# A two-layer hybrid encoder on one core: where the residual gate is applied, a branch projection by column halves, and the router's constant row

## The chip, the core and the metric

The kernel runs on one core of one Trainium2 chip. The metric is the device time of one execution, in microseconds. The core's engines work side by side, each through its own queue in order: TensorE (PE) multiplies matrices and transposes into PSUM banks, VectorE (DVE) and ScalarE (ACT) do elementwise work and move results out of PSUM, GpSimd (POOL) does elementwise work on SBUF, and SyncE (SP) issues the loads. An engine that waits holds up everything behind it in its own queue.

## The reference

Two layers, 256 tokens of 1024 channels. Each layer has a mixer and a mixture of experts; this is the part that the change touches (gt1, sc2 and sh2 come from the conditioning vector):

```python
    y_mla = mla_mixer(...) @ w_br_mla
    y_dil = dilated_mixer(dil_qkv, pos, g_q_dil, g_k_dil) @ w_br_dil
    y_win = window_mixer(win_qkv, pos, g_q_win, g_k_win, sink_win) @ w_br_win
    return (g_mla * y_mla + g_dil * y_dil + g_win * y_win) @ w_out
...
        h = rms_norm(x, g_norm1[l]) * (1 + sc1) + sh1
        x = x + gt1 * hybrid_mixer(h, pos, ...)
        h = rms_norm(x, g_norm2[l]) * (1 + sc2) + sh2
        x = x + gt2 * hier_moe(h, ...)
```

The gate gt1 is one row of 1024 values, so it may scale the columns of w_out or the product. The router takes h, and its logits h @ [w_gr, w_er] are computed as the normalised x times weights scaled by g_norm2 * (1 + sc2), plus a constant row that holds sh2 times the unscaled weights and the router's biases.

## The kernel before

Tokens lie in two tiles of 128 (t = 0, 1), channels in eight tiles of 128 (kt). A mixer is a list of jobs, each with a split and an mm part. A split takes a piece of a weight apart for three-pass multiplication: ScalarE rounds it (kh), VectorE subtracts (kl, L124 in the helper split). The mm part runs, for each token tile and column half, three matmuls: high x high, high x low, low x high. The loop at the end of mixer (L1327 to L1350) sets the order by hand: at job i it first runs the hooks registered for i, then splits some jobs ahead, then the mm part, whose last job of a product also runs its post function. An engine gets its instructions in exactly this order.

The last 18 jobs of a mixer are four for the first branch product (br0), two for the second (br1), four for the third (br2), and eight for the output projection (out); 1024 columns each, in two halves of 512 (j = 0, 1). k_jobs makes them. With halves=True the last two k-steps are run for one column half and then for the other, so that the post of half 0 runs before the matmuls of half 1 end.

- merge(br), L1139 to L1162: multiplies a branch's product by its sigmoid gate (L1156, from PSUM) and adds it into m (L1160, both inputs in SBUF). For br2 all adds are on VectorE; for br1 those of t = 0 are on GpSimd.
- start_out, L1179, a hook before the first out job: transposes all of m (L515; copies L525 on ScalarE, residual parts L526 on VectorE give mH and mL) and between the halves runs router_row (L547): eight matmuls for the constant row on all 128 partitions, an addition, and the scaling of the router weights in place (L556).
- out_gate, L1209, eight hooks from two jobs before the end of br1 on: the first makes the gate rows by gate_rows (L461: two matmuls that spread a row over the partitions, and copies, tile gtb), and each multiplies one 1024-column piece of w_out by the gate, in two GpSimd instructions (L1215).
- post_out, L1195: adds the product to x (L1205) and squares it for the norm.
- moe, L1353: transposes x (tile x2T), normalises, runs the router's logits (tile lg, 2 x 8 matmuls), and a chain of small VectorE instructions picks experts (it starts at L1375). The expert products follow.

Loads are issued by pump whenever a buffer of the ring comes free: branch weights in six units of three pieces (key bo), then the expert weights (key e).

Of the kernel before, what the change touches and what calls it, by code (L numbers as in the profile page):

```python
# [37 lines left out]
class Kern:  # L38
# [62 lines left out]
    def mm(self, out, lhsT, rhs, start, stop):  # L101
        self.nc.tensor.matmul(out, lhsT, rhs, start=start, stop=stop)  # L102
# [49 lines left out]
    def schedule(self, l):  # L152

        keys = []
        for c in range(10):
            keys += [('in', l, c)] * 4
            if c == 4:
                keys += [('uq', l)] * 4
            if c == 5:
                keys += [('ukv', l)] * 2  # L160
        first = len(keys)
        for c in range(10, 18):
            keys += [('in', l, c)] * 4
        last = len(keys)
        keys += [('bo', l, r // 3) for r in range(18)]
        if l == 0:
            keys[:12] = [keys[i] for i in self.FIRST]
        ada = [('ada', l, 1, u) for u in range(6)] + [('ada', l, 2, u) for u in range(6)]
        if l + 1 < self.layers:
            ada += [('ada', l + 1, 0, u) for u in range(6)]  # L170
        at = {}
        steps = []
        for k in ada:
            steps.append(k)
            if k[3] == 5:
                steps += [None, None]
        steps = steps[self.early(l):]
        lo, hi = 14 if l == 0 else 8, last - 5
        for n, k in enumerate(steps):
            at.setdefault(lo + n * (hi - lo) // len(steps), []).append(k)  # L180
        return keys, at
# [55 lines left out]
    def setup(self):  # L237

        nc, a, C = self.nc, self.a, self.const
        nc.scalar.preload_act_table_set(EXP_LN)  # L240
        pk = C('pk', [128, N_PK])
        nc.sync.dma_start(pk, a['pk'])
        self.ccol, self.sel4, self.cols = pk[:, 0:8], pk[:, 8:12], pk[:, 12:68].rearrange("p (l n) -> p l n", l=DEPTH)
        self.ident = pk[:, 68:196]
        self.identb = C('identb', [128, 128], BF)
        self.x = [self.alloc('w', [128, D], F32, 'x') for _ in range(2)]
        self.rows = C('rows', [128, N_ROW + DEPTH * 108])
        nc.sync.dma_start(self.rows, bass.AP(tensor=a['rows'].tensor, offset=a['rows'].offset,
                                             ap=[[0, 128], [1, N_ROW + DEPTH * 108]]))
        self.lrow = self.rows[:, N_ROW:].rearrange("p (l n) -> p l n", l=DEPTH)  # L250
        self.ipos = self.alloc('s', [128, 2 + T], I32, 'ipos')
        nc.sync.dma_start(self.ipos, a['pos'])
        for t in range(2):
            nc.sync.dma_start(self.x[t], a['x'][t])
        self.pump(2)
        self.bz0 = [self.alloc('s', [128, 512], F32, 'bz') for _ in range(2)]
        for h in range(2):
            nc.vector.memset(self.bz0[h], 0.0)
            nc.sync.dma_start(self.bz0[h][0:64:32], a['b_ada'][0, 0][h::2])
        self.sel2 = C('sel2', [128, 2])  # L260
        nc.vector.tensor_add(self.sel2, self.sel4[:, 0:2], self.sel4[:, 2:4])
        self.pump(4)
        self.load_kr(0)
        self.pump()
        nc.vector.tensor_copy(self.identb, self.ident)
        self.eps = C('eps', [128, 1])
        nc.vector.memset(self.eps, EPS)
        self.zero = C('zero', [128, 1])
        nc.vector.memset(self.zero, 0.0)

        t1 = self.small(8)
        nc.scalar.activation(t1, self.ccol, AF.Exp, scale=-1.0)
        nc.vector.tensor_scalar(t1, t1, 1.0, None, op0=ALU.add)
        nc.vector.reciprocal(t1, t1)
        self.cond = C('cond', [128, 8])
        nc.vector.tensor_mul(self.cond, t1, self.ccol)
        self.mod = {}
# [266 lines left out]
            self.free(tmp)  # L544


    def router_row(self, l):  # L547

        nc = self.nc
        ab = self.mod[l, 1]  # L550
        p = self.bank('rr')
        for kt in range(8):
            self.mm(p[:, :36], ab[:, 8 + kt:9 + kt].to_broadcast([128, 128]), self.wr[:, kt], kt == 0, kt == 7)
        self.rrow = self.cp.tile([128, 36], F32, name=f"rrow_{l}", tag='rrow')
        nc.vector.tensor_add(self.rrow, p[:, :36], self.lrow[:, l, 72:108])
        nc.vector.tensor_mul(self.wr, self.wr, ab[:, 0:8, None].to_broadcast([128, 8, 36]))  # L556
        self.free(p)

    def drain(self, g):
# [3 lines left out]
    def mixer(self, l):  # L563
# [48 lines left out]
        def k_jobs(key_of, cols, kts, lhs, post, banks, halves=False):  # L612
# [41 lines left out]
                return split, mm  # L654
            for i in range(kts):
                jobs.append(mk(i))

        self.at = 0
        att = deque()
# [412 lines left out]
        def hook(f):  # L1072
            hooks.setdefault(len(jobs), []).append(f)
# [90 lines left out]
        def bo_key(k0):  # L1164
            def f(i):
                r = k0 + i
                return ('bo', l, r // 3), (r % 3) * 1024, r % 3 == 2
            return f
# [5 lines left out]
            return f  # L1174
        k_jobs(bo_key(0), 1024, 4, lhs_o('oA', 0), merge(0), 'br0')
        k_jobs(bo_key(4), 1024, 2, lhs_o('oA', 4), merge(1), 'br1')
        k_jobs(bo_key(6), 1024, 4, lhs_o('oB', 0), merge(2), 'br2', True)

        def start_out():  # L1179
            self.free(M['oA'], M['oB'], M['G', 0], M['G', 1])  # L1180
            M['mH'] = self.alloc('u', [128, 12, 256], F32R, 'mH')
            M['mL'] = self.alloc('u', [128, 12, 256], F32R, 'mL')
            m = M['m']
            for k0 in (0, 4):
                self.transposed(lambda t, k: m[:, t, (k0 + k) * 128:(k0 + k) * 128 + 128], 4, M['mH'], M['mL'], kt0=k0)
                if k0 == 0:
                    self.router_row(l)
            self.ring = 8
            self.free(M['mg'])
        hook(start_out)  # L1190

        def lhs_m(kt, t):
            return M['mH'][:, kt, t * 128:t * 128 + 128], M['mL'][:, kt, t * 128:t * 128 + 128]

        def post_out(b, js):  # L1195
            if js == (0,):
                self.ss = self.small(4)
                self.free(*M['gt'])
            else:
                self.ring = 10  # L1200
                self.free(M['mH'], M['mL'])
            for j in js:
                for t in range(2):
                    xs = self.x[t][:, j * 512:j * 512 + 512]
                    nc.vector.tensor_add(xs, xs, b[t][j])  # L1205
                    self.squares(self.ss, t, j)
                    self.free(b[t][j])

        def out_gate(i):  # L1209
            if i == 0:  # L1210
                M['gt'] = self.gate_rows(l, 0)
            key, off, _ = bo_key(10)(i)
            u = self.take(key)[:, off:off + 1024]
            for h in range(2):
                nc.gpsimd.tensor_mul(u[:, 512 * h:512 * h + 512], u[:, 512 * h:512 * h + 512], M['gt'][h])  # L1215
        for i in range(8):
            hooks.setdefault(len(jobs) + i - 6, []).append(lambda i=i: out_gate(i))
        k_jobs(bo_key(10), 1024, 8, lhs_m, post_out, 'out', True)

        if l == 0:  # L1220
# [100 lines left out]
        for i in range(nj):  # L1321
            self.at = i
            for f in hooks.pop(i, []):
                f()
            if l == 0 and i == 5:
                next(g2)
                jobs[6][0]()  # L1327
                next(g2)
                late()
                second_half()  # L1330
                split = 9
                self.ring = 3
            while split < min(nj if i >= 5 else nfirst, i + 1 + (DEEP if i < nj - 13 else 2 if i == nj - 9 else 3)):
                jobs[split][0]()
                split += 1
            jobs[i][1]()
            if l == 0 and i in (3, 4):
                next(g2)
            if i in (nj - 11, nj - 4):
                self.load_pieces(l, 2)  # L1340
            credit += RATE
            while att and credit >= 1:
                att.popleft()()
                credit -= 1
            if not att:
                credit = 0.0
            for _ in at.get(i, []):
                next(bg)
# [4 lines left out]
    def moe(self, l):  # L1353
# [1 line left out]
        ab = self.mod[l, 1]  # L1355
        V = nc.vector
        xT = [self.alloc('w', [128, 4, 256], F32, 'x2T') for _ in range(2)]
        self.transposed(lambda t, k: self.x[t][:, k * 128:k * 128 + 128], 8, None, None, full=xT)
        xn, rs = self.norm_x('xn2', self.ss)

        pt = self.bank('lg')
        for t in range(2):
            for kt in range(8):
                self.mm(pt[:, t * 64:t * 64 + 36], xT[kt // 4][:, kt % 4, t * 128:t * 128 + 128], self.wr[:, kt], kt == 0, kt == 7)
        self.free(*xT)
        y = [[self.bank('y') for _ in range(2)] for _ in range(2)]
        for j in range(2):
# [546 lines left out]
```

## Time and profile before

| | us |
|---|---|
| median of 3 runs | 1406.43 |
| lowest and highest | 1405.89, 1408.21 |
| the profiled execution | 1407.64 |
| its span, first to last instruction | 1405.5 |
| TensorE busy in the span | 1336.0 |
| VectorE busy | 683.4 |
| ScalarE busy | 537.3 |
| GpSimd busy | 187.7 |

The profile is of one execution. The span leaves out 2.1 us of that execution's time. A matmul on fp32 data stands in the trace as more than one instruction, and consecutive matmuls overlap: an instruction that lasts 0.39 us may start 0.23 us after the one before. The layers' mixers end at 356 and 1035 us, each followed by 32 experts.

### The profile page before, as it was taken

To read this page: it belongs to the slowest core of one execution; us is meant where nothing else is said; L and a number is where in the kernel's file an instruction comes from. 1 tells how busy PE (TensorE), PEld (TensorE's weight loads), DVE (VectorE), ACT (ScalarE), POOL (GpSimd) and SP (SyncE) were. 2 spreads that over 40 slices of the span, in tenths; PEclk is the share of its full clock that TensorE was granted. 3 is DMA by queue.
4 is the path that set the end of the run, shared out by engine and by line. 5 is a ranking of instruction groups with operands and counts; after the bars stand their busy time and mean duration, and the time that the engine had idled before them with its cause. 6 is when DMAs were issued, how large, how long until landed. Compare 5 with 4: busy or idle time off the path is not lost. (4 is left out here: it accounts for less than half of the span.)

```text
span 1405.5 us, 19475 instructions
## 1 busy us (share of the span) xinstructions
PE 1336.0 (95%) x7662; PEld 877.6 (62%) x7662; DVE 683.4 (49%) x1404; ACT 537.3 (38%) x1134; POOL 187.7 (13%) x170
## 2 busy tenths in 40 slices
PE   5999999998899999999899999999889999999997
PEld 3778787887544444444368988888764444444443
DVE  5587564767623323332256775566863233233222
ACT  4555553563422222221155555456433222222211
POOL 0002064325100000000000203540810000000000
PEclk9999999999999999999999999999899999999999
DMA  9865557267689999999994526516767999999993
GB/s 375 365 248 212 196 211 291 99 270 280 232 348 427 425 425 425 425 425 425 420 414 160 203 90 259 176 76 254 270 239 289 405 425 426 425 425 426 424 424 129
DMA packets 45215, 437.95 MB, mean 312 GB/s; under 512 B 5080, under 2 KB 5608, under 8 KB 11328
## 3 DMA queue, kind: packets, MB, share of 16 engines
q1 hardware_dynamic: 44832, 435.78, 76.5%
q8 instruction: 62, 1.02, 0.3%
q0 software_dynamic: 288, 0.89, 0.2%
q14 instruction: 33, 0.27, 0.1%
HBM read 435.59 MB, written 1.05 MB: 311 GB/s over the span
## 5 line engine op out<-in xcount | busy, mean ns | idle before, releaser
L102 PE MATMUL in<-h,hH 128*128 128x384 f32 (+1 forms) x576 | 206.1, 358 | 3.7 <-ACT hH L1286 2.5
L1631 DVE TENSOR_TENSOR O<-O,gth 64x512 f32<-64x512 f32 (+1 forms) x132 | 88.8, 673 | 241.0 <-PE O L102 240.0
L102 PE MATMUL in<-h,hL 128*128 128x384 f32 (+1 forms) x576 | 195.3, 339 | 0.1
L102 PE MATMUL in<-l,hH 128*128 128x384 f32 (+1 forms) x576 | 194.6, 338 | 0.0
L1570 ACT ACTIVATE u<-A 64x384 f32<-64x384 f32 x64 | 31.1, 486 | 301.2 <-PE A L102 301.2
L102 PEld LDWEIGHTS in<-h,hH 128*128 128x128 f32 x576 | 109.1, 189 | 29.3 <-issue 18.0
L102 PEld LDWEIGHTS in<-h,hL 128*128 128x128 f32 x576 | 108.9, 189 | 1.4 <-DVE hL L1287 1.3
L102 PEld LDWEIGHTS in<-l,hH 128*128 128x128 f32 x576 | 109.3, 190 | 0.5
L1520 ACT ACTIVATE xT<-ga,modab 128x128 f32<-128x128 f32 x256 | 92.8, 467 | 21.0 <-PE ga L102 20.9
L1637 ACT ACTIVATE Op<-O 128x1024 fp32r<-128x1024 f32 x30 | 31.7, 1057 | 138.7 <-DVE O L1631 138.7
L1571 DVE SCALAR_TENSOR_TENSOR u<-A,m,u 64x384 f32<-64x384 f32 x64 | 39.4, 616 | 89.9 <-ACT u L1570 86.2
L743 POOL TENSOR_TENSOR rot<-TB,rope 128x256 f32<-128x256 f32 x8 | 11.7, 1483 | 488.4 <-ACT UC L813 429.0
L102 PE MATMUL ga<-Poh,xp 128*128 128x256 f32 x512 | 71.7, 295 | 0.0
L1540 DVE CAST PTp<-PTe 128x256 fp32r<-128x256 bf16 x32 | 13.6, 425 | 117.4 <-PE PTe L102 117.4
L102 PE MATMUL y<-Op,PTp 128*128 128x512 f32 x240 | 70.2, 415 | 0.0
L102 PEld LDWEIGHTS ga<-Poh,xp 128*128 128x128 f32 x512 | 66.0, 198 | 5.8 <-issue 4.4
L887 ACT ACTIVATE P<-P,m 128x256 f32<-128x256 f32 (+1 forms) x48 | 27.6, 576 | 79.2 <-DVE m L945 37.1
L102 PEld LDWEIGHTS y<-Op,PTp 128*128 128x128 f32 x240 | 40.6, 188 | 21.1 <-issue 15.5
L1638 DVE TENSOR_TENSOR Op<-O,Op 128x1024 fp32r<-128x1024 f32 x30 | 36.8, 1225 | 33.8 <-ACT Op L1637 29.2
L970 POOL TENSOR_SCALAR qz<-UC,gq 128x384 f32<-128x384 f32 x16 | 22.7, 1417 | 142.7 <-PE oT L102 72.6
L973 POOL TENSOR_SCALAR bias<-dist 128x128 f32<-128x128 f32 (+1 forms) x48 | 36.1, 752 | 5.2 <-PE oT L102 1.3
L102 PE MATMUL br<-kh,oA 128*128 128x512 f32 x96 | 31.3, 401 | 0.0
(845 smaller groups left out, 2532.3 us busy)
## 6 DMA issues: line engine op xcount, KB each, us to landing
piece<-in_w_e SPq DMA_DIRECT2D x12, 512.0 KB, 4.1
w('ada', 0, 0, 0)_4_90<-in_w_ada SPq DMA_DIRECT2D x1, 1536.0 KB, 9.5
w('ada', 0, 0, 1)_5_92<-in_w_ada SPq DMA_DIRECT2D x1, 1536.0 KB
w('in', 0, 0)_9_104<-in_w_in SPq DMA_DIRECT2D x2, 768.0 KB, 16.4
w('in', 0, 1)_10_108<-in_w_in SPq DMA_DIRECT2D x2, 768.0 KB, 16.3
w('in', 0, 2)_11_110<-in_w_in SPq DMA_DIRECT2D x2, 768.0 KB, 12.2
w('ada', 0, 0, 3)_18_194<-in_w_ada SPq DMA_DIRECT2D x1, 1536.0 KB
w('ada', 0, 0, 4)_35_250<-in_w_ada SPq DMA_DIRECT2D x1, 1536.0 KB
```

The lines of the kernel that those rows point to most:

```text
L102: self.nc.tensor.matmul(out, lhsT, rhs, start=start, stop=stop)
L743: g.tensor_mul(t[i], x, tab[:, i, :, None, :].to_broadcast([128, 2, nh, 16]))
L887: nc.scalar.activation(dst, src, AF.Exp, bias=mx_neg[:, i:i + 1], scale=1.0, accum_out=sm[:, i:i + 1])
L970: nc.gpsimd.tensor_scalar(qz, M['qd'][:, pr::2, t * 128:t * 128 + 128], self.gq[:, l, 1 + hh:2 + hh], None, op0=ALU.mult)
L973: nc.gpsimd.tensor_scalar(bias[:, lo:hi], self.dist[:, t, 256 + lo:256 + hi], -DIL_SLOPE[g][h], None, op0=ALU.mult)
L1520: nc.scalar.activation(dst, src, AF.Identity, scale=a2[:, kt:kt + 1], bias=s2[:, kt:kt + 1])
L1540: V.tensor_copy(PT[p], pv)
L1570: nc.scalar.activation(u[b:b + 64], A[c:c + 64, :384], AF.Silu)
L1571: V.scalar_tensor_tensor(u[b:b + 64], A[b:b + 64, :384], GC[e // 2][b:b + 64, e % 2:e % 2 + 1], u[b:b + 64], op0=ALU.mult, op1=ALU.mult)
L1631: V.tensor_mul(O[e // 2][b:b + 64, 512 * h + c:512 * h + c + n], o[c][p, :n], gt[p, c:c + n])
L1637: nc.scalar.activation(hi, whole, AF.Copy)
L1638: V.tensor_sub(lo, whole, hi)
```

## The change

Three edits. First, the gate gt1 no longer scales w_out: out_gate and its GpSimd instructions go, and post_out multiplies the product by the gate row on VectorE, from PSUM into an SBUF tile, and adds that to x. The gate rows are made later, in a hook before the second out job. Second, br2 is made by half_jobs: four jobs, of which the first two run all four k-steps for columns 0 to 511 and the last two for columns 512 to 1023; each split covers two k-steps of one half, and units 2 and 3 of the branch weights are read twice. The transposes of m are cut in two as well: the first half in the hook before the first out job, the second in the hook before the second. Splits run two jobs ahead at three jobs of br2, where it was at one. Third, the router's constant row is made on 32 partitions in moe, between the two halves of the transposes of x, and spread from one partition to all by a matmul with a row of ones and a copy on ScalarE; the scaled router weights get a tile of their own, made in the hook before the second out job.

```diff
--- before.py
+++ after.py
@@ -162,7 +162,8 @@
         for c in range(10, 18):
             keys += [('in', l, c)] * 4
         last = len(keys)
-        keys += [('bo', l, r // 3) for r in range(18)]
+
+        keys += [('bo', l, u) for u in [r // 3 for r in range(6)] + [2, 3, 3, 3] + [r // 3 for r in range(10, 18)]]
         if l == 0:
             keys[:12] = [keys[i] for i in self.FIRST]
         ada = [('ada', l, 1, u) for u in range(6)] + [('ada', l, 2, u) for u in range(6)]
@@ -267,6 +268,8 @@
         nc.vector.memset(self.eps, EPS)
         self.zero = C('zero', [128, 1])
         nc.vector.memset(self.zero, 0.0)
+        self.one = C('one', [128, 1])
+        nc.vector.memset(self.one, 1.0)
 
         t1 = self.small(8)
         nc.scalar.activation(t1, self.ccol, AF.Exp, scale=-1.0)
@@ -544,16 +547,27 @@
             self.free(tmp)
 
 
+    def router_scale(self, l):
+
+        self.wrs = self.cp.tile([128, 416], F32, name=f"wrs_{l}", tag='RT')[:, :288].rearrange("p (k n) -> p k n", k=8)
+        self.nc.vector.tensor_mul(self.wrs, self.wr, self.mod[l, 1][:, 0:8, None].to_broadcast([128, 8, 36]))
+
     def router_row(self, l):
 
         nc = self.nc
         ab = self.mod[l, 1]
         p = self.bank('rr')
         for kt in range(8):
-            self.mm(p[:, :36], ab[:, 8 + kt:9 + kt].to_broadcast([128, 128]), self.wr[:, kt], kt == 0, kt == 7)
+            self.mm(p[0:32, :36], ab[:, 8 + kt:9 + kt].to_broadcast([128, 32]), self.wr[:, kt], kt == 0, kt == 7)
         self.rrow = self.cp.tile([128, 36], F32, name=f"rrow_{l}", tag='rrow')
-        nc.vector.tensor_add(self.rrow, p[:, :36], self.lrow[:, l, 72:108])
-        nc.vector.tensor_mul(self.wr, self.wr, ab[:, 0:8, None].to_broadcast([128, 8, 36]))
+        nc.vector.tensor_add(self.rrow[0:1], p[0:1, :36], self.lrow[0:1, l, 72:108])
+        self.free(p)
+
+    def router_row_all(self):
+
+        p = self.bank('rr')
+        self.mm(p[:, :36], self.one[0:1, 0:1].to_broadcast([1, 128]), self.rrow[0:1], True, True)
+        self.nc.scalar.activation(self.rrow, p[:, :36], AF.Copy)
         self.free(p)
 
     def drain(self, g):
@@ -655,6 +669,52 @@
             for i in range(kts):
                 jobs.append(mk(i))
 
+        def half_jobs(rows, lhs, post, banks):
+
+            st = {}
+            n = len(rows) // 2
+
+            def mk(j, i):
+                def split():
+                    hi = self.alloc('w', [128, 1024], F32R, 'kh')
+                    lo = self.alloc('w', [128, 1024], F32R, 'kl')
+                    r0, r1 = rows[2 * i:2 * i + 2]
+                    if r0 // 3 == r1 // 3:
+                        cuts = [(0, 1024, r0 // 3, r0 % 3, 2)]
+                    else:
+                        cuts = [(0, 512, r0 // 3, r0 % 3, 1), (512, 1024, r1 // 3, r1 % 3, 1)]
+                    for a, b, u, k, m in cuts:
+                        key = ('bo', l, u)
+                        src = self.take(key).rearrange("p (k n) -> p k n", k=3)[:, k:k + m, 512 * j:512 * j + 512]
+                        h, w = (x[:, a:b].rearrange("p (k n) -> p k n", k=m) for x in (hi, lo))
+                        nc.scalar.activation(h, src, AF.Copy)
+                        nc.vector.tensor_sub(w, src, h)
+                        if j == 1 and k + m == 3:
+                            self.done(key)
+                    st[j, i] = (hi, lo)
+
+                def mm():
+                    if i == 0:
+                        st['b', j] = [self.bank(banks) for _ in range(2)]
+                    hi, lo = st.pop((j, i))
+                    for k in range(2):
+                        kt = 2 * i + k
+                        for t in range(2):
+                            o = st['b', j][t]
+                            h, w = lhs(kt, t)
+                            cs = slice(512 * k, 512 * k + 512)
+                            self.mm(o, h, hi[:, cs], kt == 0, False)
+                            self.mm(o, h, lo[:, cs], False, False)
+                            self.mm(o, w, hi[:, cs], False, kt == 2 * n - 1)
+                    self.free(hi, lo)
+                    if i == n - 1:
+                        o = st['b', j]
+                        post([[o[t] if x == j else None for x in range(2)] for t in range(2)], (j,))
+                return split, mm
+            for j in range(2):
+                for i in range(n):
+                    jobs.append(mk(j, i))
+
         self.at = 0
         att = deque()
 
@@ -1174,20 +1234,26 @@
             return f
         k_jobs(bo_key(0), 1024, 4, lhs_o('oA', 0), merge(0), 'br0')
         k_jobs(bo_key(4), 1024, 2, lhs_o('oA', 4), merge(1), 'br1')
-        k_jobs(bo_key(6), 1024, 4, lhs_o('oB', 0), merge(2), 'br2', True)
+        half_jobs([6, 7, 8, 9], lhs_o('oB', 0), merge(2), 'br2')
+
+        def merged(k0):
+            m = M['m']
+            self.transposed(lambda t, k: m[:, t, (k0 + k) * 128:(k0 + k) * 128 + 128], 4, M['mH'], M['mL'], kt0=k0)
 
         def start_out():
             self.free(M['oA'], M['oB'], M['G', 0], M['G', 1])
             M['mH'] = self.alloc('u', [128, 12, 256], F32R, 'mH')
             M['mL'] = self.alloc('u', [128, 12, 256], F32R, 'mL')
-            m = M['m']
-            for k0 in (0, 4):
-                self.transposed(lambda t, k: m[:, t, (k0 + k) * 128:(k0 + k) * 128 + 128], 4, M['mH'], M['mL'], kt0=k0)
-                if k0 == 0:
-                    self.router_row(l)
+            merged(0)
+
+        def rest_of_merged():
+            merged(4)
             self.ring = 8
             self.free(M['mg'])
+            M['gt'] = self.gate_rows(l, 0)
+            self.router_scale(l)
         hook(start_out)
+        hooks.setdefault(len(jobs) + 1, []).append(rest_of_merged)
 
         def lhs_m(kt, t):
             return M['mH'][:, kt, t * 128:t * 128 + 128], M['mL'][:, kt, t * 128:t * 128 + 128]
@@ -1195,26 +1261,19 @@
         def post_out(b, js):
             if js == (0,):
                 self.ss = self.small(4)
-                self.free(*M['gt'])
             else:
                 self.ring = 10
                 self.free(M['mH'], M['mL'])
             for j in js:
                 for t in range(2):
                     xs = self.x[t][:, j * 512:j * 512 + 512]
-                    nc.vector.tensor_add(xs, xs, b[t][j])
+                    gated = self.alloc('s', [128, 512], F32, 'gated')
+                    nc.vector.tensor_mul(gated, b[t][j], M['gt'][j])
+                    nc.vector.tensor_add(xs, xs, gated)
                     self.squares(self.ss, t, j)
-                    self.free(b[t][j])
-
-        def out_gate(i):
-            if i == 0:
-                M['gt'] = self.gate_rows(l, 0)
-            key, off, _ = bo_key(10)(i)
-            u = self.take(key)[:, off:off + 1024]
-            for h in range(2):
-                nc.gpsimd.tensor_mul(u[:, 512 * h:512 * h + 512], u[:, 512 * h:512 * h + 512], M['gt'][h])
-        for i in range(8):
-            hooks.setdefault(len(jobs) + i - 6, []).append(lambda i=i: out_gate(i))
+                    self.free(b[t][j], gated)
+                self.free(M['gt'][j])
+
         k_jobs(bo_key(10), 1024, 8, lhs_m, post_out, 'out', True)
 
         if l == 0:
@@ -1330,7 +1389,7 @@
                 second_half()
                 split = 9
                 self.ring = 3
-            while split < min(nj if i >= 5 else nfirst, i + 1 + (DEEP if i < nj - 13 else 2 if i == nj - 9 else 3)):
+            while split < min(nj if i >= 5 else nfirst, i + 1 + (DEEP if i < nj - 13 else 2 if nj - 12 < i < nj - 8 else 3)):
                 jobs[split][0]()
                 split += 1
             jobs[i][1]()
@@ -1355,13 +1414,16 @@
         ab = self.mod[l, 1]
         V = nc.vector
         xT = [self.alloc('w', [128, 4, 256], F32, 'x2T') for _ in range(2)]
-        self.transposed(lambda t, k: self.x[t][:, k * 128:k * 128 + 128], 8, None, None, full=xT)
+        self.transposed(lambda t, k: self.x[t][:, k * 128:k * 128 + 128], 4, None, None, full=xT)
+        self.router_row(l)
+        self.transposed(lambda t, k: self.x[t][:, 512 + k * 128:640 + k * 128], 4, None, None, full=xT[1:])
+        self.router_row_all()
         xn, rs = self.norm_x('xn2', self.ss)
 
         pt = self.bank('lg')
         for t in range(2):
             for kt in range(8):
-                self.mm(pt[:, t * 64:t * 64 + 36], xT[kt // 4][:, kt % 4, t * 128:t * 128 + 128], self.wr[:, kt], kt == 0, kt == 7)
+                self.mm(pt[:, t * 64:t * 64 + 36], xT[kt // 4][:, kt % 4, t * 128:t * 128 + 128], self.wrs[:, kt], kt == 0, kt == 7)
         self.free(*xT)
         y = [[self.bank('y') for _ in range(2)] for _ in range(2)]
         for j in range(2):
```

## Rows read from the trace of the kernel before

**Rows 1.** The page, part 1: busy time, share of the span, instructions of each engine.

```profile
PE 1336.0 (95%) x7662; PEld 877.6 (62%) x7662; DVE 683.4 (49%) x1404; ACT 537.3 (38%) x1134; POOL 187.7 (13%) x170
```

**Rows 2.** Windows, layer 0: start:end, length, busy us (instructions) per engine, PEclk, DMA share, GB/s.

```profile
304.40:305.70 1.30, 1.30 (x6) 0.58 (x4) 1.30 (x4) 0.27 (x1) 0.00 (x0) 1.00 1.02 435
...
311.60:322.95 11.35, 11.33 (x49) 8.72 (x47) 11.28 (x8) 3.42 (x5) 10.12 (x7) 1.00 0.93 365
322.95:333.80 10.85, 6.33 (x33) 6.13 (x33) 10.85 (x13) 1.67 (x3) 10.85 (x8) 0.75 0.76 281
333.80:356.46 22.66, 22.66 (x100) 18.70 (x99) 11.57 (x12) 9.55 (x13) 2.36 (x2) 0.97 0.70 262
356.46:361.80 5.34, 5.34 (x50) 5.30 (x48) 4.25 (x12) 3.29 (x9) 0.00 (x0) 1.00 0.90 327
361.80:370.84 9.04, 3.52 (x10) 1.35 (x8) 8.51 (x24) 1.39 (x2) 5.74 (x4) 0.91 0.80 303
```

**Rows 3.** Windows, layer 1, the same columns.

```profile
988.90:1000.30 11.40, 11.36 (x49) 8.74 (x47) 11.33 (x9) 3.46 (x5) 10.17 (x7) 1.00 0.93 365
1000.30:1011.56 11.26, 6.75 (x32) 6.56 (x33) 11.26 (x13) 1.66 (x3) 11.26 (x8) 0.67 0.76 283
1011.56:1034.90 23.34, 23.34 (x100) 19.18 (x99) 11.24 (x12) 9.54 (x13) 1.92 (x2) 0.94 0.66 249
```

**Rows 4.** Timeline, TensorE, layer 0: start, us, instructions, [idle before <-releaser].

```profile
326.13 0.33 PE L515 MATMUL tr<-pk,mg 128*128 128x128 f32 x1 [3.19 <-DVE mg L1160]
327.80 1.33 PE L515 MATMUL tr<-pk,mg 128*128 128x128 f32 x7 [1.34 <-DVE mg L1160]
328.93 3.46 PE L102 MATMUL rr<-wr,modab 128*128 128x36 f32 x16
```

**Rows 5.** Timeline, VectorE, the same stretch of layer 0.

```profile
316.40 6.77 DVE L124 TENSOR_TENSOR kl<-w('bo', 0, 3)_643_2926,kh 128x1024 fp32r<-128x1024 f32 x3
323.10 1.27 DVE L1156 TENSOR_TENSOR mt<-br,G 128x512 f32<-128x512 f32 x2
324.30 3.44 DVE L1160 TENSOR_TENSOR mg<-mg,mt 128x512 f32<-128x512 f32 x2
```

**Rows 6.** Timeline, GpSimd, the same stretch.

```profile
315.89 11.30 POOL L1215 TENSOR_TENSOR w('bo', 0, 4)_649_2972<-w('bo', 0, 4)_649_2972,gt 128x512 f32<-128x512 f32 x6
```

**Rows 7.** Lines L124 and L1156: count, ns min/median/max, first and last start in us, shapes.

```profile
L124 DVE TENSOR_TENSOR kl<-w('bo', 0, 4)_649_2972,kh x3: 1210/1211/1225, 336.1 to 339.1; 128x1024 fp32r<-128x1024 f32 x3
...
L1156 DVE TENSOR_TENSOR mt<-br,G x16: 673/677/679, 310.9 to 1005.6; 128x512 f32<-128x512 f32 x16
```

**Rows 8.** Windows, the experts of layer 0.

```profile
560.00:684.00 124.00, 119.64 (x690) 56.95 (x686) 36.14 (x60) 30.07 (x68) 0.00 (x0) 1.00 1.01 425
```

**Rows 9.** Timeline, TensorE and VectorE, from the output projection's end to the logits.

```profile
356.31 1.93 PE L515 MATMUL tr<-pk,x 128*128 128x128 f32 x16
358.07 3.73 PE L102 MATMUL lg<-wr,x2T 128*128 128x36 f32 x32
...
355.82 1.38 DVE L1205 TENSOR_TENSOR x<-x,out 128x512 f32<-128x512 f32 x2 [1.35 <-PE out L102]
```

**Rows 10.** Timeline, TensorE, first and last of 80 matmuls of the output projection.

```profile
337.03 0.39 PE L102 MATMUL out<-kh,mL 128*128 128x512 f32 x1
...
354.94 0.39 PE L102 MATMUL out<-kh,mH 128*128 128x512 f32 x1
```

**Rows 11.** Timeline, issue of one expert load on SyncE and its first use.

```profile
587.69 0.33 SPq L85 DMA_DIRECT2D ('e', 0, 23, 1)_992_4882<-in_w_e  x1
...
614.80 1.46 PE L102 MATMUL A<-('e', 0, 23, 1)_992_4882,xT 128*64 128x384 f32 x8
```

**Rows 12.** DMA issues: the same load, count, KB, us from issue to landing.

```profile
('e', 0, 23, 1)_992_4882<-in_w_e SPq DMA_DIRECT2D x1, 1536.0 KB, 21.3
```

**Rows 13.** Windows, the two stretches between br2 and the projection at the low clock.

```profile
328.30:335.10 6.80, 6.80 (x32) 6.59 (x31) 6.80 (x9) 2.71 (x5) 6.80 (x6) 0.50 0.64 231
1004.20:1014.40 10.20, 9.26 (x38) 8.68 (x39) 10.20 (x12) 4.24 (x6) 9.28 (x7) 0.50 0.69 245
```

## Prediction

> **What bounds the kernel now.** I read the page first: TensorE is busy for 95% of the span [rows 1], so time is to be had only where it waits or runs slowly. Then a table by windows along the way out of the mixer, in both layers. From the end of the third branch (br2) to the first matmul of the output projection, layer 0 spends 10.85 us and layer 1 11.26 us, with TensorE busy for 6.33 and 6.75 of them, while VectorE and GpSimd are busy throughout [rows 2, 3]. So this stage is bound by VectorE's queue. The timeline shows who is late: the first transpose waits 3.19 us for a merge add of L1160, the next 1.34 us for another [rows 4]. The merge adds come late because VectorE ran three splits of L124 in 6.77 us just before, and two pairs of adds at 3.44 us each after [rows 5]. GpSimd spends the same time on the gate of w_out, 11.30 us for six pieces [rows 6]. The same split takes 1.21 us where GpSimd has nothing to do, against 2.26 us here, a third of 6.77 [rows 5, 7]. Everything else on the way (the projection itself, 22.66 us, and the router's logits) is TensorE at its rate, and so is the mixture of experts behind it, where TensorE is busy for 119.64 of 124 us [rows 2, 8].
>
> **The change part by part**, per layer, with E the end of br2.
>
> 1. *The gate leaves the weights.* GpSimd loses 16 instructions. What I expect from it is not their own time, but that VectorE's instructions on two SBUF inputs fall to their free price: 1.21 us for 1024 columns, so about 0.65 for a merge add of 512 that now takes 1.72. An instruction with one PSUM input is 0.68 alone and 0.64 in a row, already now [rows 7].
>
> 2. *br2 by column halves.* The matmul count stays at 48. The first half's two products and two adds can run while TensorE does the second half. Before E VectorE now has, from about E-12 on: the second branch's merge (2.6 for the products, 0.65 to 1.3 for each of its two adds, since two adds stay on GpSimd), one split, the first half's merge (2.6), and two splits (2.4), which is 10.5 in some 12 us. So it is nearly up to date at E. After E it owes one product, two adds and the first residual part mL: 0.1 + 0.68 + 1.3 + 0.65, so the third matmul of the projection, the first that reads mL, starts at E+2.8. The eight transposes (0.12 each, from 16 in 1.93 [rows 9]) and the first two matmuls lie inside that wait. 94 matmuls remain, 0.227 us apart (79 steps from 337.03 to 354.94 [rows 10]): 21.3, and 0.2 for the last to end.
>
> 3. *Second half of the transposes and gate_rows, now behind the projection's first job.* Both are on TensorE's path: 8 x 0.12 = 1.0, and the four gate matmuls cost 1.3 where they stand now, the window from 304.40 [rows 2]. So the projection ends at E + 2.8 + 21.5 + 2.3 = E+26.6. Now it ends 33.51 us (layer 0) and 34.60 us (layer 1) after E [rows 2, 3]. The gain is 6.9 and 8.0.
>
> 4. *gate_rows leaves the first branch*: 1.3 back per layer. And br2 takes 11.35 and 11.40 us [rows 2, 3] for 48 x 0.227 + 0.2 = 11.1: 0.3 back, if its splits come in time.
>
> 5. *The gate on the product.* For the last half VectorE has four instructions instead of two. Now it starts 0.64 before the last matmul ends and is done at +0.74 [rows 9]. It will be done at -0.64 + 2 x 0.68 + 2 x 0.69 = +2.1. What waits for that is the second half of the transposes of x. For the first half of the columns the two extra instructions lie beside matmuls and cost nothing: VectorE is busy 11.57 of 22.66 us there [rows 2].
>
> 6. *router_row, now between the two halves of the transposes of x.* Its 16 instructions took 3.46 us at half clock [rows 4]. Where they stood they cost nothing, since the transposes behind them waited for VectorE anyway. Here they come at full clock, and are bounded from above by the logits' price, 32 in 3.73, so 16 in 1.9 [rows 9]; from below by half of that, as they load 32 columns instead of 128. The first transposes end at +0.8, router_row at +1.8 to +2.7, so it mostly hides behind step 5. Then come eight transposes (1.0), the one small matmul that spreads the row (0.25), and the logits (3.73): they end at +7.1 to +7.6, against +5.34 now, the window from 356.46 [rows 2]. I take 2.1 lost per layer. The normalised rows are ready before that (about +7.0), so they don't set it. The spread waits for one short add on VectorE, which stands between two copies of the transposes and has no more than those before it. The copy of the row on ScalarE delays the rstd chain by 0.2.
>
> 7. *router_scale* is the same single instruction on VectorE as now, and goes to a place where VectorE has slack: nothing. The memset of one: nothing. Unit 2 of the branch weights is held until the last split, some 5 us longer, so one expert load starts later; the loads issued here are used after the logits, some 40 us on: nothing.
>
> Sum: 6.9 + 8.0 + 2 x 1.3 + 2 x 0.3 - 2 x 2.1 = 13.9 us. I take off 0.9 for one late VectorE instruction in each layer, since step 2 leaves it only 1.5 us of room: **13.0**. The profiled execution took 1407.64 us, span 1405.5 and 2.1 around it, and is 1.2 above the median of the runs (1406.43). From the one I get 1394.6, from the other 1393.4; I forecast 1394.
>
> **Does the mixture of experts pass the gain on?** Its weights come 1.5 MB at a time, and the DMA share is 1.01 [rows 8]. The closest case I find in layer 0 is the expert weight ('e', 0, 23, 1): issued at 587.69, landed 21.3 us later at 609.0, used at 614.80, a margin of 5.8 us [rows 11, 12]. The issues themselves wait for TensorE to release buffers, so they move with it, and the margin stays unless the queue is already behind when the experts begin. Between the logits and the first expert the DMA share is 0.80 [rows 2], so the queue has room there.
>
> **The rivals.**
> *The clock.* The granted clock is 0.50 (1.2 GHz) for 6.8 us in layer 0 and for 10.2 in layer 1, from 5.4 and 3.9 us after br2's end [rows 13]. In my sum that is worth little, since most of it passes in waiting; I let it go because the new wait is under 3 us. But if the clock still falls, it falls on dense matmuls: 6.8 us at half speed is 3.4 lost in each layer, 6.8 in all, so 1401. For it: the wait is still there. Against: it is broken by transposes and two matmuls. The Trainium skill (TensorE: Matmul & The Clock Gate, What's actually happening) speaks for it: the slow clock is the default, and activity releases it, so a thin stretch would be enough. The same page (Terms) gives the penalty as the slow time times one minus the ratio. By that, as an estimate, the 17.0 us of now cost 8.5, and the sum would be some 6 us better than mine; the rows say that TensorE waited for VectorE in most of that time, so I keep to them.
> *The loads.* If the expert weights don't move with TensorE inside a layer, the gain of that layer stops at the margin of 5.8 us: 11.6 in all, 1395. If they kept their present times to the end of the program, the whole gain would stop there: 1400.6.
> *Slower.* If it isn't GpSimd that makes VectorE slow here, splits stay at 2.26 and adds at 1.72. Then VectorE has some 18 us of work in its 12 before E (6.0 + 2.3 + 4.7 + 4.6), and mL comes some 11 us after E, where the projection starts now (10.85). Steps 3 and 4 then about cancel, step 5 and 6's 2.1 is paid for nothing in layer 0 and for a little in layer 1: 3.5 in all, 1410. It decides from about E+9: with steps 3 to 6 as they are, the third matmul has to start 6.4 us later than I reckon to use up the gain. Against it is the same split at 1.21 us a few us later, in the same stage, with GpSimd idle [rows 7].
>
> **How the numbers follow.** The forecast as worked out has 0.70, the clock 0.14, the loads 0.08, slower 0.08. Range: the low end has no slip and the lower price of router_row (14.7, so 1391.7), and 1 us below that; the high end takes in the clock and the loads: 1390.5 to 1401. Under 0.2% (2.8 us) I count as no change, about what a measurement of this kernel can tell: the slower rival lies half inside that. Faster 0.92, same 0.04, slower 0.04.
>
> **What would show it.** After the change: L124 at 1.2 us throughout and L1160's adds on VectorE at about 0.65 (step 1); the first half's merge before E, and the third matmul of the projection under 3.5 us after E (step 2); the projection ending some 26.6 us after E (step 3); x done 2.1 us after the last matmul and L1375 about 7.5 us after it (steps 5, 6); the granted clock at 1.00 between br2 and the logits. It is wrong if VectorE is still busy without a pause for more than 4 us after E, if the clock falls there, if router_row waits for something, or if TensorE waits for an expert weight in either layer.

## The result, and the profile after

The changed kernel takes 1388.35 us (median; 1385.87 to 1390.37) against 1406.62 before: a ratio of 0.9867, 95% interval 0.9852 to 0.9882, or 18.3 us faster. The forecast was 13 us, and 1388.35 lies 2.1 us below the low end of its range. The profiled execution took 1390.37 us with a span of 1388.6; against the one before (1407.64, 1405.5) that is 17.3 us. The traces below are read against these 17.3.

The way out of the mixer in layer 0, as windows: start:end, length, busy us (instructions) of TensorE, weight loads, VectorE, ScalarE and GpSimd, granted clock, DMA share, GB/s. They answer to [rows 2]: br2, the wait behind it, the projection, the tail up to the logits' end, and the routing.

```profile
309.00:320.27 11.27, 11.27 (x52) 9.31 (x51) 10.24 (x13) 2.64 (x3) 1.79 (x2) 1.00 0.88 355
320.27:321.39 1.12, 0.87 (x8) 0.63 (x6) 1.12 (x3) 0.65 (x2) 0.00 (x0) 1.00 0.93 274
321.39:347.12 25.73, 25.00 (x110) 19.76 (x111) 14.05 (x18) 11.29 (x15) 0.00 (x0) 1.00 0.87 343
347.12:354.27 7.15, 6.77 (x67) 6.16 (x66) 5.58 (x15) 3.97 (x13) 0.00 (x0) 1.00 0.91 349
354.27:363.04 8.77, 3.52 (x10) 1.28 (x9) 8.24 (x25) 1.03 (x2) 5.74 (x4) 0.92 0.63 226
```

Layer 1, the end of br2, the wait and the projection, against [rows 3]:

```profile
979.50:990.66 11.16, 11.16 (x52) 9.20 (x51) 10.14 (x13) 2.65 (x3) 1.68 (x2) 1.00 0.90 358
990.66:991.79 1.13, 0.88 (x10) 0.64 (x7) 1.13 (x3) 0.65 (x2) 0.00 (x0) 1.00 0.78 239
991.79:1017.49 25.70, 24.97 (x110) 19.74 (x111) 14.04 (x18) 11.27 (x15) 0.00 (x0) 1.00 0.87 345
```

The wait of 10.85 and 11.26 us is 1.12 and 1.13 us long, the clock is 1.00 through it, and the projection ends 26.85 and 26.83 us after br2 (E+26.6 was forecast; it was 33.51 and 34.60). The VectorE timeline (start, us, instructions) shows why, beside [rows 5]: two splits of L124 in 2.36 us where three took 6.77, two adds of L1220 (before: L1160) in 1.28 where two took 3.44.

```profile
315.54 1.28 DVE L1220 TENSOR_TENSOR mg<-mg,mt 128x512 f32<-128x512 f32 x2
316.74 2.36 DVE L124 TENSOR_TENSOR kl<-w('bo', 0, 3)_643_2928,kh 128x1024 fp32r<-128x1024 f32 x2
319.62 1.37 DVE L1216 TENSOR_TENSOR mt<-br,G 128x512 f32<-128x512 f32 x2 [0.53 <-PE br L102]
320.92 1.28 DVE L1220 TENSOR_TENSOR mg<-mg,mt 128x512 f32<-128x512 f32 x2
```

TensorE at the same place, against [rows 4]: the transposes follow br2 without a wait, and the third matmul of the projection, the first that reads mL, waits 0.73 us.

```profile
320.11 1.03 PE L518 MATMUL tr<-pk,mg 128*128 128x128 f32 x8
321.39 0.50 PE L102 MATMUL out<-kh,mH 128*128 128x512 f32 x1 [0.25 <-ACT mH L528]
...
322.85 0.50 PE L102 MATMUL out<-kh,mL 128*128 128x512 f32 x1 [0.73 <-DVE mL L529]
```

Now the tail, where the prediction went astray. In the kernel before, VectorE's routing starts as the logits end, and GpSimd subtracts xlo (the low part of the normalised rows, for the gather) beside it:

```profile
361.84 0.42 DVE L1375 SCALAR_TENSOR_TENSOR L<-lg,m,rrow 128x36 f32<-128x36 f32 x2 [0.29 <-PE lg L102]
...
362.49 4.50 DVE L1402 SCALAR_TENSOR_TENSOR L<-L,rows 128x4 f32<-128x4 f32 x2
...
362.32 4.65 POOL L1380 TENSOR_TENSOR xp<-xn,xp 128x1024 fp32r<-128x1024 f32 x2 [26.16 <-ACT xp L1379]
```

After the change, the same lines under new numbers, and router_row before them, which is [rows 9] of the changed kernel:

```profile
347.92 0.71 PE L102 MATMUL rr<-wr,modab 128*32 128x36 f32 x16
...
350.18 0.41 PE L102 MATMUL rr<-rrow,one 1*128 1x36 f32 x2
350.51 3.76 PE L102 MATMUL lg<-wrs,x2T 128*128 128x36 f32 x32
...
354.96 4.13 DVE L1464 SCALAR_TENSOR_TENSOR L<-L,rows 128x4 f32<-128x4 f32 x2
...
354.43 4.65 POOL L1442 TENSOR_TENSOR xp<-xn,xp 128x1024 fp32r<-128x1024 f32 x2 [42.41 <-ACT xp L1441]
```

Two instructions on 128x4 elements last 4.50 and 4.13 us, and both times they end with GpSimd's pair (362.49 + 4.50 = 366.99 and 362.32 + 4.65 = 366.97; then 359.09 and 359.08). So in both kernels the routing seems to go on when xlo is done, not when the logits are; the runs with xlo on VectorE test it. xlo hangs on x, its norm and xhi, and ends 10.50 us after the projection before and 11.96 after: 1.46 later. The first matmul behind the routing (rk) moves with it, from 14.37 to 15.92 us after the projection in layer 0 and from 14.34 to 15.82 in layer 1.

### The profile page after: what moved, and what is told of

The parts are those of the page before. It is cut to its first block, busy times and chain, and to the rows that moved or that the text cites. A ratio compares the mean times of both kernels' runs of the same rounds, so it can differ in the third digit from the quotient of the medians.

```text
span 1388.6 us, 19465 instructions
## 1 busy us (share of the span) xinstructions
PE 1329.2 (96%) x7666; PEld 869.3 (63%) x7666; DVE 668.2 (48%) x1417; ACT 538.4 (39%) x1140; POOL 135.2 (10%) x138
## 5 line engine op out<-in xcount | busy, mean ns | idle before, releaser
L955 DVE TENSOR_SCALAR P<-P,m 128x256 f32<-128x256 f32 (+1 forms) x80 | 29.9, 407 | 1.8
```

The costliest lines, as they stand in the source:

```text
L955: nc.vector.tensor_scalar(dst, dst, r[:, i:i + 1], None, op0=ALU.mult)
```

## The experiments

Theory 1 says that GpSimd's multiplications made VectorE slow, so that taking them away is the gain, whatever order the rest stands in. Its rival, theory 2, says that the halves and the new order free VectorE's queue. For the tail, theory A says that GpSimd's xlo releases the routing, and theory B, the prediction's own, that the logits' end does. Before is 1407.63 us beside the gate alone, the halves alone, GpSimd's work in pieces of 512 and the changed kernel again, and 1407.73 beside the other four.

**The gate alone.** The kernel before with this edit:

```diff
...
-                    nc.vector.tensor_add(xs, xs, b[t][j])
+                    gated = self.alloc('s', [128, 512], F32, 'gated')
+                    nc.vector.tensor_mul(gated, b[t][j], M['gt'][j])
+                    nc.vector.tensor_add(xs, xs, gated)
...
-            for h in range(2):
-                nc.gpsimd.tensor_mul(u[:, 512 * h:512 * h + 512], u[:, 512 * h:512 * h + 512], M['gt'][h])
...
```

> The kernel before with one part of the change alone: the gate multiplies the output product (gate_rows stays at its old place, the third branch stays whole, router_row stays where it was), so GpSimd loses its 16 multiplications per layer. Theory 1 (contention: VectorE's instructions on two SBUF inputs were slow because GpSimd multiplied beside them): L124 falls from 2.26 to about 1.2 us for 1024 columns, the merge adds on VectorE from 1.72 to 0.65 to 1.3, the projection starts some 4 to 5 us earlier in each layer, the tail gains back 1.4 us of delay for the two extra instructions, and the whole is 6 to 11 us faster than before, over half of the change's 17. Theory 2 (the halves and the new order alone free VectorE's queue): the splits stay above 2 us, the whole is within 3 us of before or slower by up to 3.

Measured: 1389.16 us, ratio 0.9869 (0.9853 to 0.9886), the whole gain (the changed kernel, run beside it, takes 1389.47). My 6 to 11 us were too few, since I had given the halves the rest. TensorE behind br2 (which ends at 322.13 here):

```profile
321.97 1.03 PE L515 MATMUL tr<-pk,mg 128*128 128x128 f32 x8
322.84 1.87 PE L102 MATMUL rr<-wr,modab 128*128 128x36 f32 x16
324.55 1.07 PE L515 MATMUL tr<-pk,mg 128*128 128x128 f32 x8
325.38 0.48 PE L102 MATMUL out<-kh,mH 128*128 128x512 f32 x1
```

With VectorE at its free price there is no wait left for the halves to hide: transposes, router_row and transposes fill the 3.24 us. From the first matmul of br to the end of the projection it takes 54.54 us, and 54.34 in the changed kernel: the halves, with gate_rows and router_row at their new places, are worth 0.2 us a layer in this stretch. The tail shows the first sign against theory B: the logits end 6.70 us after the projection here (354.12 against 347.42), which is 0.46 earlier than in the changed kernel, and rk comes at 15.83, only 0.09 earlier.

**The halves alone.** The changed kernel with the gate on w_out's weights (on GpSimd) and the router as before:

```diff
...
-                    nc.vector.tensor_mul(gated, b[t][j], M['gt'][j])
-                    nc.vector.tensor_add(xs, xs, gated)
+                    nc.vector.tensor_add(xs, xs, b[t][j])
...
+            for h in range(2):
+                nc.gpsimd.tensor_mul(u[:, 512 * h:512 * h + 512], u[:, 512 * h:512 * h + 512], M['gt'][h])
...
```

> The changed kernel with the gate put back on w_out's weights on GpSimd and the router put back as before, so that the halves of the third branch (and the second half of the transposes behind the projection's first job) are the only part left. Theory 1 (contention): VectorE's splits stay near 2.2 us and its merge adds near 1.7 beside GpSimd, mL comes 7 to 11 us after the end of the third branch, and the whole is 0 to 5 us faster than before. Theory 2 (order): the third matmul of the projection starts within 4 us of the end of the third branch, and the whole is 12 us or more faster than before.

Measured: 1408.11 us, ratio 1.0005 (0.9994 to 1.0016). Theory 2 falls. VectorE and TensorE behind br2 (end at 321.32):

```profile
322.00 4.52 DVE L124 TENSOR_TENSOR kl<-w('bo', 0, 3)_643_2928,kh 128x1024 fp32r<-128x1024 f32 x2
...
327.64 3.44 DVE L1209 TENSOR_TENSOR mg<-mg,mt 128x512 f32<-128x512 f32 x2
...
331.73 0.79 PE L102 MATMUL out<-kh,mL 128*128 128x512 f32 x1 [6.37 <-DVE mL L529]
```

The third matmul comes at E+10.41: this is what my slower rival described (mL at some 11 us after E).

**The same work on GpSimd, with no data in common.** The changed kernel, with 16 multiplications of scratch tiles per layer at the old places:

```diff
...
+            for h in range(2):
+                nc.gpsimd.tensor_mul(M['pw'][0], M['pw'][0], M['pw'][1])
...
```

> The changed kernel with 16 multiplications of 512 columns per layer on GpSimd, on two scratch tiles that nothing else reads, at the places where the gate of the weights stood: the same load on GpSimd as before the change, and no data or order in common with the kernel. The output is the same. Theory 1 (contention): L124 goes back to 2.1 to 2.4 us where these run, the adds on VectorE to about 1.7, the third matmul of the projection waits 6 to 11 us after the end of the third branch, and 7 to 15 of the 17 us are lost again (1396 to 1404). Theory 2 (order): the splits stay at 1.2 us and the time within 2 us of the changed kernel's.

Measured: 1406.83 us, ratio 0.9997 (0.9988 to 1.0007): all of the gain is gone, more than the 7 to 15 us that I expected. VectorE, GpSimd and TensorE:

```profile
318.08 4.52 DVE L124 TENSOR_TENSOR kl<-w('bo', 0, 3)_643_2928,kh 128x1024 fp32r<-128x1024 f32 x2
322.53 1.27 DVE L1216 TENSOR_TENSOR mt<-br,G 128x512 f32<-128x512 f32 x2
323.73 2.35 DVE L1220 TENSOR_TENSOR mg<-mg,mt 128x512 f32<-128x512 f32 x2
...
310.67 22.43 POOL L1283 TENSOR_TENSOR pw<-pw,pw 128x512 f32<-128x512 f32 x12
...
326.73 0.79 PE L102 MATMUL out<-kh,mL 128*128 128x512 f32 x1 [5.78 <-DVE mL L529]
327.32 0.63 PE L102 MATMUL out<-kh,mH 128*128 128x512 f32 x1
```

The split is at 2.26 us again (half of 4.52; 2.30 each by itself), while L1216, which has one operand in PSUM, keeps its 0.64. Work that shares no data with the kernel brings the slowness back, so contention is shown. In layer 0 the projection ends 34.79 us after br2 instead of 26.85. Of these 7.9 us TensorE's longer wait is 5.05 (5.78 for 0.73). The other 2.9 are the clock: it is granted at 0.50 (1.2 GHz) from 322.4 to 332.7, some 5.9 us of which lie behind the wait, and there the projection's matmuls last 0.63 instead of 0.39. That is my clock rival, on the dense matmuls as it said, but with a wait of 5.78 us ahead of them and not with one of 0.73.

**The same columns in smaller pieces**, 32 multiplications of 256 columns in place of 16 of 512:

```diff
...
+            for h in range(4):
+                cs = slice(256 * (h % 2), 256 * (h % 2) + 256)
+                nc.gpsimd.tensor_mul(M['pw'][0][:, cs], M['pw'][0][:, cs], M['pw'][1][:, cs])
...
```

> The changed kernel with the same scratch columns on GpSimd as in the run with 16 multiplications of 512 columns, but cut into 32 multiplications of 256. Output as in the changed kernel. If a VectorE instruction on two SBUF operands waits for one whole GpSimd instruction and then runs at its own price (so far the addition was 1.05 us beside 512-column multiplications whatever the instruction's size: 0.65 to 1.72, 1.21 to 2.26, 0.45 to 1.46), the addition halves: L124 at 1.7 to 1.9 us, adds at 1.2, and 4 to 10 us are lost instead of 18. If the two engines share a bandwidth, L124 stays at 2.2 to 2.3 us and the time near 1407.

Measured: 1396.75 us, ratio 0.9916 (0.9900 to 0.9933), 7.3 us over the changed kernel.

The line L124 and the last two adds of L1220 in layer 0 (count, ns min/median/max, first and last start):

```profile
L124 DVE TENSOR_TENSOR kl<-w('bo', 0, 3)_643_2928,kh x2: 1755/1756/1756, 317.2 to 318.9; 128x1024 fp32r<-128x1024 f32 x2
...
L1220 DVE TENSOR_TENSOR mg<-mg,mt x2: 710/960/1211, 321.8 to 322.4; 128x512 f32<-128x512 f32 x2
```

The same adds in the run with pieces of 512:

```profile
L1220 DVE TENSOR_TENSOR mg<-mg,mt x2: 676/1212/1747, 323.7 to 324.3; 128x512 f32<-128x512 f32 x2
```

The split takes 1.756 us: 0.54 above its free 1.21, where pieces of 512 added 1.09 (2.300). Of the two adds one slips in between two of GpSimd's pieces and takes 0.71 (0.68 in the run with 512); the other takes 1.21, where it takes 1.75 beside pieces of 512. GpSimd's own pieces take 0.72 and 1.26 where nothing holds them up (the shortest of each run), some 0.17 more than what they add. So the addition is a property of GpSimd's instruction, not of VectorE's: a VectorE instruction on two SBUF operands waits for nearly one whole GpSimd instruction and then runs at its own speed. Had the two shared a bandwidth, the split would have stayed at 2.3 us, since GpSimd has no pause beside it in either run. The Trainium skill (SBUF — State Buffer, SBUF: two separate sides) says this: the pair of ports that the two engines share is "an exclusive lock, not a bandwidth split", held for the whole instruction, against VectorE instructions with two SBUF inputs. The runs agree, with 0.54 and 1.09 us.

**The changed kernel again.**

> The changed kernel itself, unaltered, to see how far its executions differ among themselves and from the first profile, which was the slowest of its four. If the 1.3 us between the profiled execution's gain (17.3) and that of the medians (18.3) are the clock's stretches falling differently from run to run, this profile has its half-clock stretches at other places than the first (361.7, 689.4, 1023.9, 1034.1, 1054.6) and its times spread over some 4 us around 1388. If the times are alike within 1 us, that reading falls.

Measured: 1389.47 us (1387.96 to 1390.51), ratio 0.9870 (0.9854 to 0.9887). The spread is 2.6 us, not 4, and the profiled execution took 1390.51, as the first. Layer 0's half-clock stretches lie at the same places; in layer 1 one is 3.4 us shorter and one has moved from 1054.6 to 1358.8. So the clock differs between executions of one kernel, but these two traces alone don't show how much it does to the time.

**router_row early.** The changed kernel, with router_row in the wait behind br2:

```diff
             merged(0)
+            self.router_row(l)
...
             merged(4)
+            self.router_row_all()
...
-        self.router_row(l)
...
-        self.router_row_all()
```

> The changed kernel with router_row put back between the two halves of the transposes of the merged rows, and its spread behind the second half; the gate and the halves stay. The logits then start about 1.0 us earlier after the last matmul of the projection (0.71 for the 16 short matmuls, 0.25 for the spread). Theory A (the routing is released by GpSimd's two subtractions of xlo, which hold the first instruction of the routing that reads two SBUF operands): the end of xlo stays at 11.9 to 12.0 us behind the projection, and rk at 15.0 to 15.9, so 0 to 0.9 us per layer is saved. Theory B (the prediction's: the logits' end sets the routing): the logits end near 6.2 us behind the projection, rk comes 1.0 us earlier and xlo's end is of no account, 2.0 us in both layers.

Measured: 1389.63 us, ratio 0.9863 (0.9847 to 0.9880): nothing. Layer 1:

```profile
1019.32 3.73 PE L102 MATMUL lg<-wrs,x2T 128*128 128x36 f32 x32
...
1023.75 4.50 DVE L1464 SCALAR_TENSOR_TENSOR L<-L,rows 128x4 f32<-128x4 f32 x2
...
1023.57 4.65 POOL L1442 TENSOR_TENSOR xp<-xn,xp 128x1024 fp32r<-128x1024 f32 x2 [42.84 <-ACT xp L1441]
```

The logits end 6.71 us after the projection, about half a us earlier than in layer 0 of the changed kernel (7.16; its layer 1 has 7.77, with the clock at half from 1023.9 on) and not at the 6.2 of theory B, since their transposes wait for x anyway. The pair on 128x4 lasts 4.50 us instead of 4.13, so the earlier start is given back, and rk comes at 15.72 (15.82 in the changed kernel). Ahead of it the projection ends 27.37 us after br2 instead of 26.83, since router_row now stands in TensorE's way. In its layer 0 the clock was at half and the logits ended at 8.86, 2.15 us later than in layer 1; rk came at 15.95. The logits' end moves by 2.15 us and the routing by 0.23: theory B falls.

**xlo on VectorE**, behind the first one-hot of the gather, instead of on GpSimd beside the routing:

```diff
-            nc.gpsimd.tensor_sub(xlo[t], xn[t], xhi[t])
...
         onehot(0)
+        for t in range(2):
+            V.tensor_sub(xlo[t], xn[t], xhi[t])
```

> The changed kernel with the two subtractions of xlo on VectorE behind the first one-hot instead of on GpSimd beside the routing. Theory A (GpSimd's xlo holds the routing): the pair of L1464 that took 4.13 us falls to about 0.4, rk comes 12.0 to 12.6 us behind the projection instead of 15.9, and after paying up to 1.7 us where the gather waits for xlo, 2.0 to 3.7 us per layer are saved: 4 to 7 us in all. Theory B (the logits' end and the routing's own instructions set it): rk stays where it is, xlo on VectorE adds 2.4 us to the path, and the whole is 1 to 5 us slower than the changed kernel.

Measured: 1383.41 us (1382.29 to 1387.29), ratio 0.9835 (0.9818 to 0.9852), faster than the changed kernel by 6.1 us by the medians. VectorE and TensorE in layer 0:

```profile
354.11 0.36 DVE L1462 SCALAR_TENSOR_TENSOR L<-L,rows 128x4 f32<-128x4 f32 x2
...
359.71 2.35 DVE L1728 TENSOR_TENSOR xp<-xn,xp 128x1024 fp32r<-128x1024 f32 x2
...
358.47 0.28 PE L102 MATMUL rk<-Mb,tri 128*128 128x32 bf16 x5
...
360.99 0.50 PE L102 MATMUL ga<-Poh,xp 128*128 128x256 f32 x2 [0.92 <-DVE xp L1728]
362.12 1.80 PE L102 MATMUL ga<-Poh,xp 128*128 128x256 f32 x13 [0.63 <-DVE xp L1728]
```

The pair takes 0.36 us, rk comes 12.21 us after the projection in place of 15.92, and the gather waits 0.92 and 0.63 us for xlo. Theory A is shown, and this version beats both kernels.

**The gate alone and xlo on VectorE**, both edits on the kernel before:

> The kernel before with the gate on the output product (the third branch whole, router_row at its old place) and with xlo on VectorE behind the first one-hot. By theory A the two gains add, 18 us for the gate and 4 to 7 us for xlo: 1382 to 1386 us. By theory B it is as slow as the gate alone or slower, 1389 to 1394 us.

Measured: 1384.58 us (1382.05 to 1385.31), ratio 0.9831 (0.9815 to 0.9847). The two edits add, and without halves and without the router's move the kernel is as fast as with them.

## Why the prediction was right and wrong

*Step 1* was right and is the whole cause of the gain: L124 at 1.22 us, two adds at 1.28. *Step 2* was right in its times (third matmul at E+2.58, 2.8 forecast), but the halves were not needed for it: alone they bring nothing, and the gate alone brings as much as the whole change. *Steps 3 and 4*: from the first matmul of br to the end of the projection the profiled pair gains 8.76 us in layer 0 (63.10 to 54.34) and 9.86 in layer 1 (64.19 to 54.33), where my sum without the slip has 6.9 + 1.3 + 0.3 = 8.5 and 9.6. That is 0.5 us more in all. By parts, step 4 had too little (2.1 us a layer up to the end of br2 instead of 1.6) and step 3 a little too much (6.7 and 7.8 instead of 6.9 and 8.0). *The slip* of 0.9 us for a late VectorE instruction did not come: TensorE's wait of 0.73 us for mL was already in E+2.8.

*Step 5* was right: x is done 2.1 us after the last matmul (349.21 against 347.12). *Step 6* is the step whose mechanism failed. It was right on the logits in layer 0 (7.16 us after the projection; 7.1 to 7.6 forecast; 7.77 in layer 1, at the lower clock), and wrong in its conclusion that their end sets the tail. I priced the two layers at 2.1 each from the logits' end and set the normalised rows aside as "ready before that". They are (6.54 us after the projection in layer 0), but what is made of them, xhi and then xlo, goes on to 11.96 us and holds VectorE. So the tail loses 1.55 and 1.48 us instead of 2.1 each, about as much as xlo comes later (1.46): 1.2 us less in all than I took off. I had the mechanism from [rows 5, 7] and looked for it in one stage only; the 9.04 us between logits and rk stood in [rows 2] with GpSimd busy for 5.74 of them.

The sum with these three terms is 13.0 + 0.5 + 0.9 + 1.2 = 15.6, and the profiled pair shows 17.3. Of the difference 0.6 us lies ahead of the first branch of layer 0 (293.37 to 292.77), where nothing is removed; in the other runs this point lies between 291.46 and 293.86 us. 0.4 lies around the span, and 1.0 between rk and the first expert of layer 1 (5.84 to 4.85). That 1.0 is the clock, a term that the sum doesn't have. The stretch from rk to the first expert, layers 0 and 1 before, then layers 0 and 1 after, in the columns of [rows 2]:

```profile
370.84:376.43 5.59, 5.59 (x26) 3.81 (x25) 3.65 (x21) 3.32 (x8) 0.00 (x0) 0.53 0.01 3
1049.24:1055.08 5.84, 5.84 (x25) 3.97 (x25) 3.87 (x23) 3.57 (x8) 0.00 (x0) 0.50 0.00 0
...
363.04:368.74 5.70, 5.70 (x26) 3.92 (x26) 3.63 (x21) 3.42 (x8) 0.00 (x0) 0.52 0.01 4
1033.31:1038.16 4.85, 4.85 (x26) 3.49 (x26) 3.48 (x20) 3.10 (x7) 0.00 (x0) 0.65 0.33 133
```

In all the runs with xlo on GpSimd this stretch takes 3.94 to 3.96 us at a granted clock of 1.00, 4.73 to 4.88 at 0.64 to 0.68, and 5.59 to 5.84 at 0.50 to 0.53. Layer 0 has the low clock before and after and gains nothing there. Both traces of the changed kernel have 0.65 in layer 1; of the kernel before there is one trace, so whether the change brings this 1.0 us is open. The medians show 1.0 us more than the profiled pair, and what that is no run settles: the profiled executions were the slowest of their kernel, twice. The range failed for the terms: 15.6 from the median of before is 1390.8, at its very end, and it had no room for the other 2.7 us of the medians' 18.3.

*The rivals.* The clock did not fall between br2 and the logits, in either layer; in layer 1 it fell 1.4 us before the logits' end. It did fall where TensorE waited longer: in layer 0 around waits of 5.78 and 2.72 us (GpSimd's scratch work, in large and in small pieces), not around the 0.73 of the changed kernel. The loads: the expert weight with the least margin lands 3.9 us ahead of its use (5.8 before), and nothing waited for it. Slower: GpSimd's scratch work makes the case where VectorE stays slow, and gives 1406.83 us, where I had 1410.

## What to carry to other kernels

Before moving a step off TensorE's path, look at what GpSimd does while VectorE is late: a VectorE instruction with two SBUF operands paid here for nearly a whole GpSimd instruction, whatever its own size, so the small ones in a serial chain (here 128x4) pay most. Search every stage for it, not only the one that the change is in, and ask of each wait which instruction on another engine ends within some 0.02 us of it. And when an edit does several things, cost each one as if it stood alone: here the gate alone carried the gain.

## What the runs showed of the hardware

- The addition to a VectorE instruction on two SBUF operands beside GpSimd follows GpSimd's piece: 1.09 us at 512 columns, 0.54 at 256, and 1.6 to 2.2 us each for the pair on 128x4 beside two subtractions of 1024 columns (4.13 to 4.50 us where 0.36 is the free price). Instructions with an operand in PSUM (L1216, 0.64) did not change, nor did the one reduction with a single SBUF operand that stands beside xlo (L1462, 0.16 us, as in the run with xlo on VectorE).
- 16 matmuls with 32 stationary columns took 0.71 us (router_row after), and 16 with 128 took 1.87 at full clock (the gate alone), which is less than half; my bounds were 1.0 and 1.9.
- The same stretch of work (rk to the first expert) took 3.95 us at the full clock and 5.8 with all of it at 1.2 GHz.
